# A mixer, cross-attention and feed-forward layer on one core: the last two quarters' output projection starts before the last mixer is done, and the feed-forward's token combinations are made later

## The chip, the cores and the metric

The kernel runs on one core of one Trainium2 chip. The metric is the time of one execution in device microseconds (us); lower is better. The core has a tensor engine (PE, with its weight loads shown as PEld), a vector engine (DVE), a scalar engine (ACT), GpSimd (POOL, nearly unused here) and SyncE (SP), whose queue issues all DMAs of this kernel. Each engine takes its own instructions in order and waits where one needs a result of another engine.

## What is computed

One layer of a decoder on 2048 tokens of 1024 channels, in float32. A mixer (a gated linear recurrence, "lru", beside a convolution module, "conf") feeds one output projection; then come cross-attention to 256 memory tokens and a gated feed-forward with a short convolution.

```
h = rms_norm(x, mix_norm_g);  z = h @ w_in
lru_x, lru_gate, conf_a, conf_b = split(z)                 # 512 channels each
y_lru = rg_lru(causal_dwconv(lru_x, 4 taps)) * gelu(lru_gate)
c = causal_dwconv(conf_a * sigmoid(conf_b), 31 taps)
c = silu(layer_norm(c))
x = x + concat([y_lru, c]) @ w_out
h = rms_norm(x, xa_norm_g);  m = rms_norm(mem, mem_norm_g)
x = x + softmax(h @ w_q @ k.T / 16) @ v @ w_o              # 4 heads, k and v from m @ w_kv
h = rms_norm(x, ffn_norm_g);  g, u = split(h @ w_up)       # 3072 channels each
x = x + (gelu(causal_dwconv(g, 3 taps)) * u) @ w_down
return rms_norm(x, final_norm_g)
```

## The kernel before

The tokens are cut into four quarters of 512 (q = 0 to 3; `TT` = 512, `NTB` = 4 blocks of 128 tokens). Every product is made of three matmuls on operands that are split into a high and a low part (names that end in h and l: `wh`, `wl`, `xh`, `xl`), each matmul 128x128 by 512 columns.

Per quarter there is a mixer (`mixer`, with `mix_norm`, `conf` and `lru`): normed tokens are turned by transposes against `ident`, multiplied by `W_in` (matmuls of `xh`, `xl` with `wh`, `wl`), and the gated product goes into `cb`, on which DVE runs 30 convolution steps (`conv<-cb`) for each of four channel blocks, 120 in all per quarter. The recurrence has its two gates (`gwa`, `gwx`), a scan, and its own convolution (`xc`). `normed` then does the layer norm over the 512 channels of `conv` (`conf_out`): a first sum (`sum<-sum,conv`) and a sum of squares (`sum<-sum,sq`), each followed on PE by one product with `ones`, a square root on ACT, and a `RECIPROCAL` of 512 columns on DVE.

Quarters 0 and 1 go through `attend` one by one: output projection (`yh`, `yl`), scores against the folded memory matrix (`xah`, `xal`), softmax (`prob`), and the second product (`pth`, `ptl`). Quarters 2 and 3 are done together by `attend_pair`, which makes each of its three products as a seven-step product of 2x2 blocks (`Folded.run`, after Strassen and Winograd; its seven steps are called products below). The rows of the blocks are the two quarters, the inner halves are lru and conf channels. The first two products (n = 0 and 1, operands A11 and A12) use quarter 2 alone; the third (n = 2, operand S2 = A21 + A22 - A11) is the first to use quarter 3. PE names their operands `hidh` and `hidl`. Sums of weight blocks for it are made on DVE by `Folds.prepare` (`wd<-wh,wl` and `t<-wd`), with `FOLD_PACE`.

The feed-forward's up product is of the same kind over token halves. For the first half of the tokens, `HalfX.kept` loads normed tokens (`xn`), makes four combinations of each of four channel blocks on DVE (16 instructions, `t<-xn` and `t<-xn,t`), and stores them.

What sets the order: each part is a generator that records operations and yields a pause, in units of PE work recorded so far; `drive` steps the first task in the list `TURNS` that is due. A planner (`Program.emit`) then gives every operation a due time, worked back from PE's recorded order, simulates the engines with a table of costs, and writes out a fixed order for each engine. So a pause (`MIX_WAIT`, `MIX_PACE`, `ATT_PACE`, `FOLD_PACE`, `T_PACE`, the numbers in `NORMED`) or a place in `TURNS` moves instructions on all engines at once. PE has eight banks (`ps`) to write to.

Of the kernel before, what the change touches and what calls it, by code (L numbers as in the profile page):

```python
# [23 lines left out]
NQ = S // TT  # L24
# [393 lines left out]
def hybrid_layer(  # L418
# [350 lines left out]
    def conf(X, C, pb, row, pace):  # L769
        for c in (0, 2):  # L770
            if pb is None:
                pb = yield from project(W_in, 3 * DL + c * P, X, pace)
            sg = []
            for j in range(2):
                t = tmp("sg")
                ACT(t[:], scaled("sg", pb[j], row)[:], AF.Sigmoid)
                sg.append(scaled("sg", t, row))
            pb = None
            yield 0
            pa = yield from project(W_in, 2 * DL + c * P, X, pace)  # L780
            cbs = []
            for j in range(2):
                cb = pr.new("D", (P, CK - 1 + TT), name="cb")
                V("tensor_copy", cb[:, : CK - 1], ctail[c + j][:])
                V("tensor_tensor", cb[:, CK - 1 :], pa[j][:], sg[j][:], op=ALU.mult)
                V("tensor_copy", ctail[c + j][:], cb[:, TT : TT + CK - 1])
                cbs.append(cb)
            for j in range(2):
                a, cb, w = tmp("conv"), cbs[j], vec["v512"][:, c + j, :]
                ACT(a[:], cb[:, 0:TT], AF.Identity, scale=w[:, I_CCW : I_CCW + 1], bias=w[:, I_CCB : I_CCB + 1])  # L790
                for t in range(1, CK):
                    V("scalar_tensor_tensor", a[:], cb[:, t : t + TT], w[:, I_CCW + t : I_CCW + t + 1], a[:], op0=ALU.mult, op1=ALU.add)
                C.append(a)
            yield 0
# [36 lines left out]
    def lru(q, X, L, row, pace):  # L831
        for c in (0, 2):
            pz = yield from project(W_in, c * P, X, pace)
            H = []
            for j in range(2):
                w = vec["v512"][:, c + j, :]
                zt = ztail[c + j]
                xc, z = tmp("xc"), scaled("z", pz[j], row)
                ACT(xc[:], z[:], AF.Identity, scale=w[:, I_LCW + 3 : I_LCW + 4], bias=w[:, I_LCB : I_LCB + 1])
                if row is None and q in Z_COPIED:  # L840
                    z = tmp("z")
                    ACT(z[:], pz[j][:], AF.Copy)
                for s in range(1, LK):
                    wt = w[:, I_LCW + 3 - s : I_LCW + 4 - s]
                    V("scalar_tensor_tensor", xc[:, s:], z[:, : TT - s], wt, xc[:, s:], op0=ALU.mult, op1=ALU.add)
                    V("scalar_tensor_tensor", xc[:, :s], zt[:, LK - 1 - s :], wt, xc[:, :s], op0=ALU.mult, op1=ALU.add)
                V("tensor_copy", zt[:], z[:, TT - LK + 1 :])
                H.append(xc)
            yield GATES
            for j in range(2):  # L850
                w = vec["v512"][:, c + j, :]
                xc = H[j]
                rt = []
                xh, xl = pair("x")
                split(xc[:], xh, xl)
                cs = slice((c + j) * P, (c + j + 1) * P)
                for (gh, gl), bi in zip(gates, (I_BA, I_BX)):
                    p = ps()
                    with together():
                        mm3(p[:], gh[:, cs], gl[:, cs], xh[:], xl[:], True, True)  # L860
                    t = tmp("gate")
                    ACT(t[:], p[:], AF.Sigmoid, bias=w[:, bi : bi + 1])
                    rt.append(t)
                r, i = rt
                V("tensor_tensor", i[:], i[:], xc[:], op=ALU.mult)
                a, m = xc, tmp("m")
                sp = nsp[:, c + j : c + j + 1]
                ACT(a[:], r[:], AF.Exp, scale=sp)
                ACT(r[:], r[:], AF.Tanh, scale=sp)
                ACT(m[:], a[:], AF.Square)  # L870

                V("scalar_tensor_tensor", m[:], m[:], 1.0, r[:], op0=ALU.add, op1=ALU.mult)
                ACT(m[:], m[:], AF.Sqrt, scale=-1.0)
                V("tensor_tensor", i[:], i[:], m[:], op=ALU.mult)
                V("tensor_tensor_scan", r[:], a[:], i[:], hlast[c + j][:], op0=ALU.mult, op1=ALU.add)
                V("tensor_copy", hlast[c + j][:], r[:, TT - 1 : TT])
                H[j] = r
            pg = yield from project(W_in, DL + c * P, X, pace)
            for j in range(2):
                ge = tmp("gelu")  # L880
                ACT(ge[:], scaled("gelu", pg[j], row)[:], AF.Gelu_apprx_tanh)
                V("tensor_tensor", ge[:], H[j][:], ge[:], op=ALU.mult)
                if q in FOLDED:
                    L.append(ge)
                    continue
                hi, lo = pair("y")
                split(ge[:], hi, lo)
                L.append((hi, lo))
            yield 0
# [156 lines left out]
    mixed = [None] * NQ  # L1046
    started = [Task(None) for _ in range(NQ)]
    attended = [Task(None) for _ in range(NQ)]
    turned_x = [Task(None) for _ in range(NQ)]
    x2_kept = Kept("x2", NQ * NTB * 2, F32)  # L1050
    xn_kept = Kept("xn", NQ * NK, F32)

# [12 lines left out]
    def mixer(q, after):  # L1065
        if after:
            yield after
            yield MIX_WAIT[q]
        if q == 0:
            X, pb, row = yield from first_tokens()  # L1070
        else:
            X, pb, row = (yield from mix_norm(q)), None, None
        C, L = [], []
        yield from conf(X, C, pb, row, MIX_PACE[q])
        yield from lru(q, X, L, row, MIX_PACE[q])
        del X, row
        mixed[q] = C, L

    def first_tokens():

# [182 lines left out]
    class HalfX:  # L1263
# [14 lines left out]
        def kept(self, ready, wait):  # L1278

            keys = ("T2", "T1", "T3", "T4")  # L1280
            k = Kept(f"tx{self.h}", 4 * KH, F32)
            yield ready
            for i in range(KH):
                b = {key: self.one(key, i) for key in ("B11", "B12", "B22")}
                t1 = combine("t", b["B12"][:], b["B11"][:], ALU.subtract)
                t2 = combine("t", b["B22"][:], t1[:], ALU.subtract)
                k.put(i, t2[:])
                k.put(KH + i, t1[:])
                yield wait
                t3 = combine("t", b["B22"][:], b["B12"][:], ALU.subtract)  # L1290
                t4 = combine("t", self.one("B21", i)[:], t2[:], ALU.subtract)
                k.put(2 * KH + i, t3[:])
                k.put(3 * KH + i, t4[:])
                del b, t1, t2, t3, t4
                yield wait
            for n, key in enumerate(keys):
                self.t[key] = lambda n=n: [k.get(n * KH + i) for i in range(KH)]
# [354 lines left out]
                yield from self.step(n, banks, start, into)  # L1652
                after(n)

    def attend_pair(ready):
        for t in ready:
            yield t
        q0 = FOLDED[0]
# [1 line left out]
        src = {}  # L1660
        x1_kept = Kept("x1", 4 * NTB, F32)

        def nothing(n):
            return ()

        def residual(load, store, st):
            acc = {}
# [34 lines left out]
        def operands(th):  # L1702
            Y, L = mixed[q0 + th]
            src[th, 0], src[th, 1] = L, Y

        operands(0)
        operands(1)
        st1 = [Stats(), Stats()]
        acc, add = residual(load_one, lambda th, tb, half, t: x1_kept.put((th * NTB + tb) * 2 + half, t[:]), st1)
        xsrc, posts = {}, [None, None]  # L1710
# [12 lines left out]
                posts[th] = spawn(normalise(acc, th, st1, PAIR_WAIT[0], take_xa(th)), me)  # L1723

        yield F_out.done
        yield from Folded(src, F_out, add).run(nothing, after1)
        del acc, add


# [128 lines left out]
        vec["v3072"] = columns([ffn_conv_w[0], ffn_conv_b], DFF, "v3072")  # L1858

    EARLY, VO_WAIT, V_LATE, Z_COPIED = 5, 2, 500, (0, 1)  # L1860
    MIX_WAIT, MIX_TURN, LN_SUM, LN_SQ, GATES = (1, 13, 0, 0), 6, 7, 1, 4
    MIX_PACE, ATT_PACE = (0, 4, 6, 4), ((0, 3, 0), (0, 0, 6), (7, 1, 1), (4, 0, 6))
    PAUSE = 2
    MEM_WAIT, VO_LATE, ATT_TURN, FFN_TURN, X_PACE, T_PACE = 0, 11, 1, (5, 0, 17, 5), 6, 2

    FOLDED = (2, 3)
    PAIR_WAIT, PAIR_TURN, FOLD_PACE = (1, 0, 9, 15), 5, (15, 6, 40)
    EARLY_AT = 4
    FOLD_AT = lambda: ([turned_x[0]], [mem_a, turned_x[1]], [mem_vo])
    F_out, F_a, F_vo = Folds(W_out, "t_out"), Folds(A_rows, "t_a"), Folds(VO_rows, "t_vo")  # L1870

    NORMED = [lambda: ([m[0]], 111), lambda: ([attended[0]], 33), lambda: ([m[2]], 2), lambda: ([m[3], n[2]], 0)]
    ATTEND = [lambda: [n[0]], lambda: [n[1]]]
    TURNS = lambda: [later, m[0], first_t, m[3], n[1], first, mem_a, fold, m[1], a[0], n[0], mem_vo, m[2], n[2], n[3], a[1], a[2], tail]
    X = [HalfX(h) for h in range(NH)]

    def first_x():
# [26 lines left out]
    m, n, a = mixers, normeds, attends  # L1904
# [3 lines left out]
        if q not in FOLDED:  # L1908
            a[q].gen = attend(q, ATTEND[q]())
    a[3] = a[2]  # L1910
    a[2].gen = attend_pair([n[2], n[3], attended[1]])
    fold = Task(fold_weights())
    later.gen, mem_a.gen, mem_vo.gen = setup_later(), memory_a(), memory_vo()
    first_t.gen, first.gen, tail.gen = X[0].kept(a[1], T_PACE), first_x(), feed_forward()
# [34 lines left out]
```

## Time and profile before

| | |
|---|---|
| median of 3 runs | 2457.88 us (2457.01 to 2458.15) |
| the profiled execution | 2455.91 us |
| its span, first to last instruction | 2454.1 us |
| mean granted PE clock | 0.996 |
| PE busy | 99% of the span, 11068 instructions |
| DVE busy | 80% |
| ACT busy | 51% |
| DMA | 566.78 MB, 231 GB/s in the mean |

The span holds, in order: the first three mixers with the memory products and the first quarter's attention (to about 650 us), the last mixer among the second quarter's second product (to about 823 us), the pair of quarters 2 and 3 (to about 1072 us), and the feed-forward. A busy PE is not PE at its peak, since its matmuls are pipelined; a place where it is held up shows in the view of waits, in the start times of the timeline, or as a stretch in which PE's count is low. Nearly all instructions are recorded through one helper, so the line is L394 everywhere, and the names of the tiles tell the place.

### The profile page before, as it was taken

How to read it: one execution, taken by the hardware profiler on the slowest of the kernel's cores; microseconds unless marked ns; L12 is line 12 of the kernel's file. 1: busy time of each engine (PE TensorE's matmuls, PEld its weight loads, DVE VectorE, ACT ScalarE, POOL GpSimd, SP SyncE). 2: the span in 40 equal slices, each digit the busy share in tenths (PEclk: the TensorE clock that was granted, in tenths of full speed). 3: DMA queues.
4: the chain of work that ended last, by engine and by line, in shares of the span. 5: the costliest groups of instructions: out<-in, count | busy, mean ns of one | idle time of the engine just before them, and what ended most of it. 6: DMA issues, size and time to landing. Idle time of an engine off the chain costs nothing. (4 is left out here: it accounts for less than half of the span.)

```text
span 2454.1 us, 33077 instructions
## 1 busy us (share of the span) xinstructions
PE 2422.9 (99%) x11068; PEld 2014.0 (82%) x11068; DVE 1974.7 (80%) x3297; ACT 1248.6 (51%) x2189; POOL 0.7 (0%) x6
## 2 busy tenths in 40 slices
PE   9999999999999799999999999999999999999998
PEld 8898888888787688888888888888888888888887
DVE  7999994399789978879888788987886675667656
ACT  6762665335925678685545445555454431225223
POOL 0000000000000000000000000000000000000000
PEclk9999999999999899999999999999999999999999
DMA  9688688786886965877554455444542487779775
GB/s 321 212 296 326 204 296 286 255 298 224 311 276 206 315 231 194 284 274 254 200 202 171 149 178 180 163 172 151 184 149 83 125 293 252 255 252 353 237 254 176
DMA packets 340416, 566.78 MB, mean 231 GB/s; under 512 B 32988, under 2 KB 110812, under 8 KB 340246
## 3 DMA queue, kind: packets, MB, share of 16 engines
q1 hardware_dynamic: 340246, 564.68, 67.4%
q8 instruction: 87, 1.43, 0.2%
q14 instruction: 83, 0.68, 0.1%
HBM read 403.07 MB, written 161.48 MB: 230 GB/s over the span
## 5 line engine op out<-in xcount | busy, mean ns | idle before, releaser
L394 PE MATMUL ps<-Xh,wh 128*128 128x512 f32 x1344 | 523.0, 389 | 0.0
L394 PE MATMUL ps<-Xl,wh 128*128 128x512 f32 x1344 | 522.9, 389 | 0.0
L394 PE MATMUL ps<-Xh,wl 128*128 128x512 f32 x1344 | 522.8, 389 | 0.0
L394 PE MATMUL ps<-wh,hidh 128*128 128x512 f32 x1008 | 394.2, 391 | 0.0
L394 PE MATMUL ps<-wl,hidh 128*128 128x512 f32 x1008 | 392.9, 390 | 0.0
L394 PE MATMUL ps<-wh,hidl 128*128 128x512 f32 x1008 | 392.8, 390 | 0.0
L394 DVE SCALAR_TENSOR_TENSOR conv<-cb,v,conv 128x512 f32<-128x512 f32 x480 | 339.5, 756 | 2.4 <-ACT conv L394 1.3
L394 PEld LDWEIGHTS ps<-Xh,wh 128*128 128x128 f32 x1344 | 252.3, 188 | 52.6 <-DVE up L394 0.2
L394 PEld LDWEIGHTS ps<-Xl,wh 128*128 128x128 f32 x1344 | 252.3, 188 | 52.5
L394 PEld LDWEIGHTS ps<-Xh,wl 128*128 128x128 f32 x1344 | 252.2, 188 | 52.3
L394 DVE TENSOR_TENSOR acc<-acc,ps 128x512 f32<-128x512 f32 x224 | 151.0, 687 | 152.3 <-PE ps L394 149.6
L394 PEld LDWEIGHTS ps<-wh,hidh 128*128 128x128 f32 x1008 | 189.7, 188 | 39.9 <-ACT gelu L394 0.5
L394 PEld LDWEIGHTS ps<-wl,hidh 128*128 128x128 f32 x1008 | 189.6, 188 | 39.7 <-issue 0.5
L394 PEld LDWEIGHTS ps<-wh,hidl 128*128 128x128 f32 x1008 | 189.6, 188 | 39.5
L394 PE MATMUL ps<-xh,wh 128*128 128x512 f32 x512 | 203.5, 397 | 0.0
L394 PE MATMUL ps<-xh,wl 128*128 128x512 f32 x512 | 199.5, 390 | 0.0
L394 PE MATMUL ps<-xl,wh 128*128 128x512 f32 x512 | 199.4, 389 | 0.0
L394 ACT ACTIVATE hidh<-s 128x512 fp32r<-128x512 f32 x144 | 87.8, 630 | 189.1 <-DVE s L394 134.3
L394 ACT ACTIVATE wh<-s 128x512 fp32r<-128x512 f32 x192 | 119.7, 628 | 107.7 <-DVE s L394 80.3
L394 ACT ACTIVATE wh<-raw 128x512 fp32r<-128x512 f32 x208 | 127.9, 627 | 74.1 <-PE ps L394 32.2
L394 DVE TENSOR_TENSOR wl<-raw,wh 128x512 fp32r<-128x512 f32 x208 | 141.8, 692 | 20.0 <-ACT wh L394 18.3
L394 ACT ACTIVATE u<-ps 128x512 f32<-128x512 f32 x144 | 85.9, 597 | 135.7 <-PE ps L394 133.7
(239 smaller groups left out, 3884.8 us busy)
## 6 DMA issues: line engine op xcount, KB each, us to landing
raw<-in_w_up_dram SPq DMA_DIRECT2D x96, 512.0 KB
wh<-w_down SPq DMA_DIRECT2D x164, 256.0 KB
wl<-w_down SPq DMA_DIRECT2D x164, 256.0 KB
wh<-w_in SPq DMA_DIRECT2D x96, 256.0 KB
wl<-w_in SPq DMA_DIRECT2D x96, 256.0 KB
hid<-cv SPq DMA_DIRECT2D x48, 512.0 KB
h<-hid SPq DMA_DIRECT2D x96, 256.0 KB
w_down<-wh SPq DMA_DIRECT2D x84, 256.0 KB
```

The lines of the kernel that those rows point to most:

```text
L394: getattr(e, name)(*[resolve(a) for a in args], **{k: resolve(a) for k, a in kw.items()})
```

## The change

`attend_pair` is released when quarter 2 is normed and quarter 1 attended; it waits for mixers 2 and 3 and for quarter 3's `normed` only before its third product (`more`, in `before1`). `HalfX.kept` of the first half waits in addition until the pair reaches its seventh product (`pair_begun`, set at `KEPT_AT` = 6). `mixer` publishes its lists C and L before they are filled, so that the parts are at hand as they are made. `convolved` is set but read nowhere. Beside these, the pauses and the list `TURNS` have new values: `m[3]` stands third in the list, `n[3]` and `n[2]` ahead of `fold`, `T_PACE` is 10 for 2, `FOLD_PACE` (7, 4, 33) for (15, 6, 40), and so on. The number of instructions is unchanged on PE, DVE and SP; on ACT 6 fewer table loads stand in the program (72 for 78).

```diff
@@ -1046,7 +1046,8 @@
     mixed = [None] * NQ
     started = [Task(None) for _ in range(NQ)]
     attended = [Task(None) for _ in range(NQ)]
-    turned_x = [Task(None) for _ in range(NQ)]
+    turned_x, convolved = ([Task(None) for _ in range(NQ)] for _ in range(2))
+    pair_begun = Task(None)
     x2_kept = Kept("x2", NQ * NTB * 2, F32)
     xn_kept = Kept("xn", NQ * NK, F32)
 
@@ -1070,11 +1071,10 @@
             X, pb, row = yield from first_tokens()
         else:
             X, pb, row = (yield from mix_norm(q)), None, None
-        C, L = [], []
+        C, L = mixed[q] = [], []
         yield from conf(X, C, pb, row, MIX_PACE[q])
+        convolved[q].done = True
         yield from lru(q, X, L, row, MIX_PACE[q])
-        del X, row
-        mixed[q] = C, L
 
     def first_tokens():
 
@@ -1280,6 +1280,8 @@
             keys = ("T2", "T1", "T3", "T4")
             k = Kept(f"tx{self.h}", 4 * KH, F32)
             yield ready
+            if not self.h:
+                yield pair_begun
             for i in range(KH):
                 b = {key: self.one(key, i) for key in ("B11", "B12", "B22")}
                 t1 = combine("t", b["B12"][:], b["B11"][:], ALU.subtract)
@@ -1652,7 +1654,7 @@
                 yield from self.step(n, banks, start, into)
                 after(n)
 
-    def attend_pair(ready):
+    def attend_pair(ready, more):
         for t in ready:
             yield t
         q0 = FOLDED[0]
@@ -1660,8 +1662,13 @@
         src = {}
         x1_kept = Kept("x1", 4 * NTB, F32)
 
-        def nothing(n):
-            return ()
+        def before1(n):
+            if n == 2:
+                for t in more:
+                    yield t
+                operands(1)
+            if n == KEPT_AT:
+                pair_begun.done = True
 
         def residual(load, store, st):
             acc = {}
@@ -1704,7 +1711,6 @@
             src[th, 0], src[th, 1] = L, Y
 
         operands(0)
-        operands(1)
         st1 = [Stats(), Stats()]
         acc, add = residual(load_one, lambda th, tb, half, t: x1_kept.put((th * NTB + tb) * 2 + half, t[:]), st1)
         xsrc, posts = {}, [None, None]
@@ -1723,7 +1729,7 @@
                 posts[th] = spawn(normalise(acc, th, st1, PAIR_WAIT[0], take_xa(th)), me)
 
         yield F_out.done
-        yield from Folded(src, F_out, add).run(nothing, after1)
+        yield from Folded(src, F_out, add).run(before1, after1)
         del acc, add
 
 
@@ -1858,20 +1864,20 @@
         vec["v3072"] = columns([ffn_conv_w[0], ffn_conv_b], DFF, "v3072")
 
     EARLY, VO_WAIT, V_LATE, Z_COPIED = 5, 2, 500, (0, 1)
-    MIX_WAIT, MIX_TURN, LN_SUM, LN_SQ, GATES = (1, 13, 0, 0), 6, 7, 1, 4
-    MIX_PACE, ATT_PACE = (0, 4, 6, 4), ((0, 3, 0), (0, 0, 6), (7, 1, 1), (4, 0, 6))
+    MIX_WAIT, MIX_TURN, LN_SUM, LN_SQ, GATES = (0, 9, 5, 0), 4, 5, 0, 5
+    MIX_PACE, ATT_PACE = (2, 4, 3, 4), ((1, 3, 0), (0, 0, 0), (10, 0, 4), (2, 4, 2))
     PAUSE = 2
-    MEM_WAIT, VO_LATE, ATT_TURN, FFN_TURN, X_PACE, T_PACE = 0, 11, 1, (5, 0, 17, 5), 6, 2
+    MEM_WAIT, VO_LATE, ATT_TURN, FFN_TURN, X_PACE, T_PACE = 18, 11, 1, (4, 6, 4, 11), 3, 10
 
     FOLDED = (2, 3)
-    PAIR_WAIT, PAIR_TURN, FOLD_PACE = (1, 0, 9, 15), 5, (15, 6, 40)
-    EARLY_AT = 4
+    PAIR_WAIT, PAIR_TURN, FOLD_PACE = (0, 0, 9, 15), 7, (7, 4, 33)
+    EARLY_AT, KEPT_AT = 6, 6
     FOLD_AT = lambda: ([turned_x[0]], [mem_a, turned_x[1]], [mem_vo])
     F_out, F_a, F_vo = Folds(W_out, "t_out"), Folds(A_rows, "t_a"), Folds(VO_rows, "t_vo")
 
-    NORMED = [lambda: ([m[0]], 111), lambda: ([attended[0]], 33), lambda: ([m[2]], 2), lambda: ([m[3], n[2]], 0)]
+    NORMED = [lambda: ([m[0]], 108), lambda: ([attended[0]], 30), lambda: ([m[2]], 19), lambda: ([m[3], n[2]], 4)]
     ATTEND = [lambda: [n[0]], lambda: [n[1]]]
-    TURNS = lambda: [later, m[0], first_t, m[3], n[1], first, mem_a, fold, m[1], a[0], n[0], mem_vo, m[2], n[2], n[3], a[1], a[2], tail]
+    TURNS = lambda: [later, m[0], m[3], first_t, mem_a, n[1], n[3], n[2], fold, m[1], a[0], n[0], mem_vo, first, m[2], a[1], a[2], tail]
     X = [HalfX(h) for h in range(NH)]
 
     def first_x():
@@ -1908,7 +1914,7 @@
         if q not in FOLDED:
             a[q].gen = attend(q, ATTEND[q]())
     a[3] = a[2]
-    a[2].gen = attend_pair([n[2], n[3], attended[1]])
+    a[2].gen = attend_pair([n[2], attended[1]], [m[2], m[3], n[3]])
     fold = Task(fold_weights())
     later.gen, mem_a.gen, mem_vo.gen = setup_later(), memory_a(), memory_vo()
     first_t.gen, first.gen, tail.gen = X[0].kept(a[1], T_PACE), first_x(), feed_forward()
```

The order of instructions moves throughout the first 1100 us. Three places follow.

PE, at the layer norm of quarter 3. Before, the two products with `ones` stood in a row behind the last input matmuls of mixer 3, and ahead of the pair's first product:

```order
L394 MATMUL ps<-xh,wl 128x512
L394 MATMUL ps<-sum,ones 128x512 x2
L394 MATMUL ps<-wh,hidh 128x512
L394 MATMUL ps<-wl,hidh 128x512
L394 MATMUL ps<-wh,hidl 128x512
```

In the change they stand apart, among the second quarter's second product. The first of them:

```order
L394 MATMUL ps<-wl,pth 128x512
L394 MATMUL ps<-wh,ptl 128x512
L394 MATMUL ps<-sum,ones 128x512
L394 MATMUL ps<-wh,pth 128x512
L394 MATMUL ps<-wl,pth 128x512
```

And the pair's first product, behind the last of that product's matmuls:

```order
L394 MATMUL ps<-wh,pth 128x512
L394 MATMUL ps<-wl,pth 128x512
L394 MATMUL ps<-wh,ptl 128x512
L394 MATMUL ps<-wh,hidh 128x512
L394 MATMUL ps<-wl,hidh 128x512
```

Between the first and the second product with `ones` stand 36 matmuls of `pth` and `ptl` now, and between the second and the pair's first product 54.

DVE, at the last sums of squares of quarter 3 (`sum<-sum,sq`). Before, the token combinations stood right behind them, and eight more of them ahead:

```order
L394 TENSOR_TENSOR sum<-sum,sq 128x512
L394 TENSOR_TENSOR hidl<-gelu,hidh 128x512
L394 TENSOR_TENSOR sum<-sum,sq 128x512
L394 TENSOR_TENSOR hidl<-gelu,hidh 128x512
L394 TENSOR_TENSOR sum<-sum,sq 128x512
L394 TENSOR_TENSOR t<-xn 128x512
L394 TENSOR_TENSOR t<-xn,t 128x512
L394 TENSOR_TENSOR t<-xn 128x512
L394 TENSOR_TENSOR t<-xn,t 128x512 x2
L394 TENSOR_TENSOR hidl<-conv,hidh 128x512 x4
L394 TENSOR_TENSOR t<-xn,t 128x512
L394 RECIPROCAL r<-r 128x512
```

In the change none stands there; the sum of a residual and the splits of gated products are between them, and the first token combination comes some 90 rows later:

```order
L394 TENSOR_TENSOR sum<-sum,sq 128x512
L394 TENSOR_TENSOR x_5015<-x_5015,ps 128x512
L394 TENSOR_TENSOR sum<-sum,sq 128x512
L394 COPY hlast<-gate 128x1
L394 TENSOR_TENSOR gelu<-gate,gelu 128x512
L394 TENSOR_TENSOR sum<-sum,sq 128x512
L394 TENSOR_TENSOR hidl<-gelu,hidh 128x512 x2
L394 COPY hlast<-gate 128x1
L394 TENSOR_TENSOR wd<-wh,wl 128x512
L394 COPY ctail<-cb 128x30
L394 TENSOR_TENSOR t<-wd,t 128x512
```

PE, at the end of the second quarter's score product. Before, the 32 transposes of mixer 3's tokens stood there:

```order
L394 MATMUL ps<-wh,xal 128x512
L394 MATMUL ps<-ident,x 128x128 x32
L394 MATMUL ps<-sum,ones 128x512
L394 MATMUL ps<-xh,wh 128x512
L394 MATMUL ps<-xl,wh 128x512
```

In the change those transposes stand among the second quarter's first output projection, and between the score product and the softmax's transposes stand 24 input matmuls of mixer 3, with 24 more behind:

```order
L394 MATMUL ps<-xl,wh 128x512
L394 MATMUL ps<-xh,wl 128x512
L394 MATMUL ps<-ident,prob 128x128 x16
L394 MATMUL ps<-xh,wh 128x512
L394 MATMUL ps<-xl,wh 128x512
```

## The prediction

> **What bounds the kernel now.** The page comes first: TensorE (PE) is shown busy for 99% of the span.
>
> ```profile
> span 2454.1 us, 33077 instructions
> PE 2422.9 (99%) x11068; PEld 2014.0 (82%) x11068; DVE 1974.7 (80%) x3297; ACT 1248.6 (51%) x2189; POOL 0.7 (0%) x6
> ```
>
> By this row at most 2454.1 - 2422.9 = 31.2 us could go, and the number of matmuls does not change. So the question is where PE is held up, and which of these places the new order touches. The view of stretches tells them apart; its columns are length, then busy time and count for PE, PEld, DVE, ACT and POOL, then PE's granted clock, DMA share and GB/s.
>
> ```profile
> 51.40:650.00 598.60, 597.22 (x2875) 501.34 (x2876) 509.64 (x892) 330.06 (x589) 0.00 (x0) 1.00 0.78 271
> 689.35:822.69 133.34, 118.09 (x530) 96.65 (x528) 132.27 (x222) 67.30 (x103) 0.00 (x0) 0.96 0.75 257
> 822.69:860.00 37.31, 37.17 (x150) 29.74 (x151) 37.31 (x60) 19.58 (x35) 0.00 (x0) 0.93 0.84 285
> 830.00:2440.00 1610.00, 1610.00 (x7202) 1335.86 (x7201) 1257.20 (x2035) 776.09 (x1350) 0.00 (x0) 1.00 0.62 209
> ```
>
> The first 650 us and everything from 830 us on are full. In 689 to 823 us the vector engine (DVE) is full instead (132.3 of 133.3 us) and PE is not. That is the last mixer's stretch. PE's waits there, and in the stretch of 640 to 660 us before it (last two rows), are these:
>
> ```profile
> PE ps L394 <- DVE sum L394: 11.6, 1, 11.6
> PE ps L394 <- ACT xn L394: 2.0, 4, 1.1
> PE ps L394 <- DVE xl L394: 1.3, 1, 1.3
> PE ps L394 <- DMA wh<-VO: 1.9, 1, 1.9
> PE ps L394 <- ACT prob L394: 1.8, 3, 0.9
> ```
>
> The Trainium skill ("Trainium Kernel Development and Optimization", Performance Expectations) holds that busy time of matmuls is a poor measure, because they are pipelined, and that weight-load busy time is a good one. Here weight loads fill 1335.86/1610 = 83% of the undisturbed stretch and 82% of the span; by that rule an estimate of the loss is 2454.1 - 2014.0/0.83 = 28 us, close to what is counted below.
>
> **Term 1, the last mixer's stretch.** PE's and DVE's groups in 689.3 to 822.7 us, and DVE's first and last instruction in it:
>
> ```profile
> L394 PE MATMUL ps<-xh,wh 128*128 128x512 f32 x100 | 39.4, 394 | 0.0
> L394 PE MATMUL ps<-wh,pth 128*128 128x512 f32 x52 | 20.3, 391 | 0.0
> L394 PE MATMUL ps<-ident,xn 128*128 128x128 f32 x32 | 6.0, 335 | 2.2 <-ACT xn L394 2.0 <-ACT gate L394 0.2
> L394 PE MATMUL ps<-xh,gwah 128*128 128x512 f32 x4 | 1.7, 417 | 0.2 <-ACT xh L394 0.2
> L394 DVE SCALAR_TENSOR_TENSOR conv<-cb,v,conv 128x512 f32<-128x512 f32 x120 | 82.6, 749 | 0.8 <-ACT conv L394 0.7
> ...
> 689.35 0.69 DVE L394 TENSOR_TENSOR cb<-ps,sg 128x512 f32<-128x512 f32 x1 [7.50 <-PE ps L394]
> 821.99 0.70 DVE L394 TENSOR_TENSOR sum<-sum,sq 128x512 f32<-128x512 f32 x1
> ```
>
> DVE waits 7.50 us for the first gated product of the last mixer, then works without a break for 133.3 us until the last sum of squares, for which PE is waiting. PE's own work in that time is smaller. Matmuls of 512 columns start 0.23 us apart, transposes some 0.11 us (16 in 1.91 us, the last one's end included), a DVE tensor-tensor step takes 0.60 us, a convolution step up to 0.69 (82.6/120 above), a row maximum 0.69:
>
> ```profile
> 774.57 0.39 PE L394 MATMUL ps<-xh,wh 128*128 128x512 f32 x1
> 774.80 0.39 PE L394 MATMUL ps<-xl,wh 128*128 128x512 f32 x1
> 775.26 1.91 PE L394 MATMUL ps<-ident,xn 128*128 128x128 f32 x16
> 810.16 1.02 PE L394 MATMUL ps<-sum,ones 128*128 128x512 f32 x2
> 646.77 0.69 DVE L394 TENSOR_REDUCE smalls<-ps 128x2 f32<-128x512 f32 x1
> 823.79 0.70 DVE L394 TENSOR_TENSOR t<-xn 128x512 f32<-128x512 f32 x1
> 824.39 1.30 DVE L394 TENSOR_TENSOR t<-xn,t 128x512 f32<-128x512 f32 x2
> ```
>
> In the old order there stand 300 input-projection matmuls, 156 of the second quarter's last product (pth, ptl) and 24 of the gates: 480 x 0.227 = 109.0 us. With 48 transposes (5.3) and one sum (0.9) it is 115.2 us. PE loses 133.3 - 115.2 = 18.1 us.
>
> In the new order mixer 3 starts earlier, so the same stretch, from its first gated product to the second sum, holds 300 + 180 (score product, xa) + 138 (pth, ptl) + 24 = 642 matmuls, 145.7 us; with 32 transposes (3.5) and a sum (0.9) 150.1 us. DVE's share grows too, from 221 instructions to 262. Out go 8 token combinations (t<-xn), 4 residual sums, 2 splits; in come 13 more weight sums (wd), 12 more differences of these, 4 more splits, 2 more gate products: 17 x 0.60 = 10.2 us; 8 row maxima add 5.4 and 16 small ones some 1.6. So DVE needs 133.3 + 17.2 = 150.5 us against PE's 150.1: the debt of 18.1 us falls to 0.4. But the balance is even, so each wait of DVE in this stretch now comes through to PE. Lower bound 0, where DVE's surplus is hidden by small waits of PE elsewhere. Upper bound from the softmax, whose instructions now stand inside the stretch and waited like this before it:
>
> ```profile
> 642.57 0.17 DVE L394 TENSOR_TENSOR smalls<-smalls 128x4 f32<-128x4 f32 x1 [3.96 <-ACT junk L394]
> 652.99 0.17 DVE L394 RECIPROCAL smalls<-smalls 128x2 f32<-128x2 f32 x1 [1.15 <-ACT prob L394]
> 654.66 0.75 DVE L394 SCALAR_TENSOR_TENSOR xl<-ps,v,xh 128x512 fp32r<-128x512 f32 x1 [0.92 <-ACT xh L394]
> ```
>
> With the smaller ones between them this is about 8 us. I take 3.0 us, nearer the low end, since the new order puts convolution steps between the softmax's steps, which the old one had not there. Term 1: -18.1 + 3.0 = -15.1.
>
> **Term 2, the slow restart.** After the wait of 11.65 us the matmuls come at half pace:
>
> ```profile
> 822.83 2.04 PE L394 MATMUL ps<-sum,ones 128*128 128x512 f32 x2 [11.65 <-DVE sum L394]
> 823.89 1.41 PE L394 MATMUL ps<-wh,hidh 128*128 128x512 f32 x1
> ...
> 828.39 0.40 PE L394 MATMUL ps<-wh,hidh 128*128 128x512 f32 x1
> ```
>
> Ten matmuls, nine steps in 4.50 us where 2.04 would do: 2.5 us lost, the clock of 0.93 in the third stretch. No wait of 1 to 2 us shows this. With term 1's wait it goes: -2.5. The Trainium skill ("TensorE: Matmul & The Clock Gate", Part 1) has an idle window of some 3.4 us halve the clock and about as much busy time restore it; that would price the restart at 3.4 x 0.5 = 1.7 us, an estimate that would put the result 0.8 us higher. The trace agrees in kind, with 2.5 us; by that rule, too, a remaining wait of 3 us in one piece costs no restart.
>
> **Term 3, the transposes at 650 us.** They wait three times for softmax results, then for weights:
>
> ```profile
> 650.21 1.91 PE L394 MATMUL ps<-ident,x 128*128 128x128 f32 x16
> 658.26 1.13 PE L394 MATMUL ps<-sum,ones 128*128 128x512 f32 x2 [1.94 <-DMA wh<-VO]
> 658.82 0.79 PE L394 MATMUL ps<-xh,wh 128*128 128x512 f32 x1
> 659.45 0.40 PE L394 MATMUL ps<-xl,wh 128*128 128x512 f32 x1
> ```
>
> 32 transposes need 3.5 of the 8.05 us between the first two rows: 4.5 lost, and 0.4 more at the step of 0.63. In the new order mixer 3's transposes are done long before, among the first output projection. Behind the score product stand 24 input matmuls (5.4 us) before the softmax's transposes, and 24 more behind those. So -4.9, and 0.5 back for the new place (0 to 4.9).
>
> **Parts that I cost at nothing.** The pair's first two products no longer wait for mixer 3, but product 3, which does, stands behind 54 + 96 matmuls and 32 transposes, 37.6 us after the second sum (old: 96 matmuls, 21.8). DVE's way from the last sum of squares to the fourth split of the S2 operands ends here:
>
> ```profile
> 845.41 1.90 DVE L394 TENSOR_TENSOR hidl<-s,hidh 128x512 fp32r<-128x512 f32 x3
> ```
>
> From 822.7 to 847.3 that was about 25 us; it has two instructions more now, 1.2 us: some 11 us of cover. If that cover went, the excess would come as a wait before product 3. The 16 token combinations move behind, into the pair's later products: 9.6 us of DVE, where DVE is full until 860 us but has an eighth to a quarter of its time free after:
>
> ```profile
> 850.00:900.00 50.00, 50.00 (x238) 41.83 (x237) 44.18 (x77) 34.60 (x72) 0.00 (x0) 1.00 0.86 291
> 900.00:950.00 50.00, 50.00 (x238) 41.93 (x237) 37.32 (x67) 40.02 (x83) 0.00 (x0) 1.00 0.49 158
> ```
>
> Without cover they cost up to 9.6 us. Their loads and stores on SP's queue number as before. The other moves (memory products and W_out among the second mixer, to 640 us) stay in a stretch that loses little either way: +0.5, within -3 to +4.
>
> **Sum.** 2454.1 - 15.1 - 2.5 - 4.9 + 0.5 + 0.5 = 2432.6 us of span. The median of the runs lies 3.8 us over the span: 2436.4, and I say 2436.5.
>
> **Rivals.** (a) The debt moves rather than goes: DVE's waits in the softmax come through whole, 8 us in place of 3, and in a piece long enough for a slow restart (2.5): 2436.5 + 5 + 2.5 = 2444. For it speaks the even balance of 150.5 against 150.1; against it that convolution steps are at hand to fill. (b) Everything small goes as well: no wait in the stretch, and 3 us of those in the first 640: 2436.5 - 6 = 2430.5. (c) The change does not do what it says: the sum is still late by as much, since some chain that ACT or DMA sets, not DVE's work, ended that wait. Then 2457. Against it: DVE has 132.27 busy of 133.34 us. (d) Slower: DVE takes its instructions in order, and 15 weight sums that need fresh loads now stand among the convolutions; each blocks them if its load is late. Waits for such loads are these, the first over the whole span, the second in 560 to 900 us:
>
> ```profile
> DVE t L394 <- DMA wd<-in_w_out_dram: 14.8, 3, 7.3
> DVE wd L394 <- DMA wl<-A: 0.3, 1, 0.3
> ```
>
> At 7.3 us each, four make 29 us on top of the even balance in place of 3, and with the restart kept (2.5) the run takes 2436.5 + 26 + 2.5 = 2465. It decides from about 22 us of such waits on; the second row, the same kind of sum in the same phase, speaks against it.
>
> **Chances.** Forecast 0.70, (a) 0.14, (b) 0.07, (c) 0.03, (d) 0.06. The range reaches from (b) past (a), 2430 to 2448; the ends of the unknown costs, 3 us down and 8 up, lie inside. A change of 0.2% (5 us) is about what this measurement can tell: faster 0.91, the same 0.03, slower 0.06.
>
> **What would show it.** Right: no PE wait over 3 us behind the sums of mixer 3, no matmuls at 0.43 us behind them, the granted clock at 1.00 there, DVE full through this stretch, and fewer transposes that wait for prob. The weakest step is the 3.0 us: a longer wait at mixer 3's sums or at the transposes of the second quarter's probabilities means (a). A wait at product 3, for s or hid, would show that the later coverage is wrong. DVE waits for DMA before wd mean (d). A gain under 15 us would say that the stretch was not bound by DVE's amount of work.

## The result, and the profile after

| | before | after |
|---|---|---|
| median of 4 runs each | 2457.45 us (2455.34 to 2458.15) | 2430.69 us (2430.26 to 2433.14) |
| the profiled execution | 2455.91 us | 2431.12 us |
| its span | 2454.1 us | 2429.3 us |
| mean granted PE clock | 0.996 | 0.999 |

The changed kernel is faster: ratio 0.9895, 95% interval 0.9877 to 0.9912, 26.8 us between the medians. The page's head shows the same work in a shorter span (PE still busy for 99%):

```profile
span 2429.3 us, 33082 instructions
PE 2415.3 (99%) x11068; PEld 2010.7 (83%) x11068; DVE 1970.7 (81%) x3297; ACT 1241.7 (51%) x2183; POOL 0.7 (0%) x6
```

Stretches of the changed kernel (columns as in the prediction). The first runs from the last mixer's first gated product to the second sum, the second is what follows that sum:

```profile
635.88:785.01 149.13, 146.99 (x660) 120.80 (x659) 148.78 (x265) 69.43 (x127) 0.00 (x0) 1.00 0.77 263
785.01:822.00 36.99, 36.99 (x179) 30.84 (x178) 31.74 (x54) 29.34 (x54) 0.00 (x0) 1.00 0.88 293
```

The last mixer's stretch is 149.13 us long, DVE is still full in it (148.78), and now PE is nearly full too (146.99; before 118.09 of 133.34). Behind the sum the granted clock is 1.00 where it was 0.93. What is left of PE's waits, in the whole execution (two more are of 0.5 us and less):

```profile
PE ps L394 <- DMA raw<-in_ffn_norm_g_dram: 3.3, 1, 3.3
PE ps L394 <- DVE ptl L394: 1.9, 1, 1.9
PE ps L394 <- ACT mem L394: 1.3, 1, 1.3
```

The row `DVE sum` of 11.6 us is gone, and so are the rows for `xn` and `prob`. PE's timeline at the two sums of the last layer norm has no idle time before either:

```profile
775.83 1.12 PE L394 MATMUL ps<-sum,ones 128*128 128x512 f32 x2
...
785.01 1.02 PE L394 MATMUL ps<-sum,ones 128*128 128x512 f32 x2
```

They stand 9.2 us apart, and 36 matmuls fill that time (8.2 us at 0.227, and 0.9 for the sum). Before they stood at 810.16 and 822.83 us, 12.7 apart, with nothing between them. This distance turned out to be the largest single part of the matter.

### The profile page after: what moved, and what is told of

It reads as the page before. It is cut to its first block, busy times and chain, and to the rows that moved or that the text cites. A ratio compares the mean times of both kernels' runs of the same rounds, so it can differ in the third digit from the quotient of the medians.

```text
span 2429.3 us, 33082 instructions
## 1 busy us (share of the span) xinstructions
PE 2415.3 (99%) x11068; PEld 2010.7 (83%) x11068; DVE 1970.7 (81%) x3297; ACT 1241.7 (51%) x2183; POOL 0.7 (0%) x6
## 5 line engine op out<-in xcount | busy, mean ns | idle before, releaser
L394 DVE TENSOR_TENSOR wl<-s,wh 128x512 fp32r<-128x512 f32 x192 | 131.7, 690 | 30.2 <-ACT wh L394 21.4
```

The source lines that it names most:

```text
L394: getattr(e, name)(*[resolve(a) for a in args], **{k: resolve(a) for k, a in kw.items()})
```

## The experiments

The names: `old_...` is the kernel before with an edit, `new_...` the changed kernel with one. In all of them the kernel before ran beside; its medians were 2456.4 to 2457.4 us.

**1. Is the old order bound by DVE's amount of work?** `old_less_conv` skips 27 of the last mixer's 120 convolution steps as the program is written out, and leaves the order as it is (these values are then missing from the output).

```diff
+                if o.mark and o.mark * 9 % 40 < 9:
+                    continue
```

> The old order with 27 of the last mixer's 120 convolution steps left out (that part of the result is then not computed); every other instruction and the order of all engines as before. Theory (amount of DVE work between the last mixer's first gated product and its last sum of squares sets PE's wait): DVE's 133.3 us shrink by 27 x 0.66 = 17.9 us to PE's own 115.2, the slow restart (2.5 us) goes too, and 3 to 6 us come back before the pair's third product: 2442 us, 2437 to 2447. Rival (that wait is ended by a chain over ACT or a transfer, DVE only looks full): within 3 us of the old kernel's 2457.

Measured: 2457.46 us (2453.96 to 2462.41), ratio 1.0000 (0.9991 to 1.0010). The rival's number. 27 x 0.69 = 18.6 us of DVE work are gone, and PE waits as long for the sum. Its view of waits:

```profile
PE ps L397 <- DVE sum L397: 11.1, 1, 11.1
```

And a stretch of the mixer in which DVE was busy for 20.00 of 20 us before:

```profile
720.00:740.00 20.00, 20.00 (x90) 16.57 (x89) 16.57 (x27) 1.63 (x2) 0.00 (x0) 1.00 0.56 196
```

So the theory of the prediction fell for the old order: DVE's full 133 us were real, but they were not what kept PE waiting.

**2. Does DVE's amount bind in the new order?** `new_dose12` and `new_dose40` put 12 and 40 clears of a spare tile behind every tenth and every third convolution step of the last mixer; `new_less_conv` leaves out the same 27 steps as above.

```diff
+                if o.mark and o.mark * 1 % 10 < 1:
+                    self.nc.vector.memset(self.extra_tile[:], 0.0)
```

> The changed kernel with 12 clears of an unused tile of 128x512 (0.40 us each, 4.8 us in all) spread over the last mixer's convolution steps on DVE; nothing else moves. In the changed kernel's trace DVE is full from 635.9 to 784.1 us and PE takes the second product with ones 0.9 us after the last sum of squares. Theory (even balance): all but 0.9 us comes through, 3.5 to 5 us slower, 2434 to 2436. Rival (DVE has room there): under 1.5 us.

> As the dose of 12, with 40 clears, 16.1 us of DVE work. Theory: 15 us come through, and a wait that long in one piece brings the slow restart (2.5 us) again if it is not cut up into short waits: 2445 to 2449. Rival: under 5 us, since the planner left slack between the sums and the third product.

> The changed kernel with 27 of the last mixer's 120 convolution steps left out (that part of the result is then not computed). Theory: only the wait for ptl (1.9 us) and a gate wait of 0.2 still hang on DVE there: 1.5 to 3 us faster, 2428 to 2429. Rival (the stretch still holds a debt that is spread in small waits): 8 us or more faster.

Measured: 2436.48 (2436.02 to 2437.74), 2448.32 (2448.17 to 2451.36) and 2429.36 us (2429.04 to 2429.63): +5.8, +17.6 and -1.3 against the change's 2430.69. The first and the last lie just outside what was expected. On DVE the stretch from the first gated product to the last sum of squares takes 148.4 us in the change, and 153.3 and 165.6 with the clears, so the doses are 4.9 and 17.3 us: added work comes through about one to one, removed work gives little. PE does not lose this time at the sums (`new_dose12` has no wait there) but in waits spread over the stretch and in slow matmuls behind them. The new order stands close to the balance of the two engines that the prediction worked out.

**3. What ends the wait in the old order?** Between the first sum and the second stands a chain: the mean is taken off four blocks (`conv<-conv,ps`), ACT squares them, DVE adds the squares. DVE's timeline of the kernel before in that time:

```profile
811.83 0.68 DVE L394 TENSOR_TENSOR conv<-conv,ps 128x512 f32<-128x512 f32 x1
812.43 1.29 DVE L394 SCALAR_TENSOR_TENSOR m<-m,gate 128x512 f32<-128x512 f32 x2
813.63 1.88 DVE L394 TENSOR_TENSOR conv<-conv,ps 128x512 f32<-128x512 f32 x3
815.42 0.69 DVE L394 TENSOR_TENSOR hidl<-gelu,hidh 128x512 fp32r<-128x512 f32 x1
816.03 1.30 DVE L394 TENSOR_TENSOR gate<-gate,m 128x512 f32<-128x512 f32 x2
817.23 2.46 DVE L394 TENSOR_TENSOR_SCAN gate<-xc,hlast,gate 128x512 f32<-128x512 f32 x2
819.60 0.68 DVE L394 TENSOR_TENSOR sum<-sum,sq 128x512 f32<-128x512 f32 x1
```

From 811.83 to the last sum's end at 822.69 it is 10.9 us, all of it full on DVE: 7 steps of the chain itself (7 x 0.60 = 4.2), and 6.7 of the recurrence and of splits that stand among them in DVE's order. PE has nothing in its order for that time. The new theory: **PE waits because its two sums stand next to each other, as long as this chain takes**; what DVE did earlier counts only where it makes the first sum late. Three runs tried it, all without the 27 steps, so that DVE's amount ahead of the first sum is out of the way (values are missing from the output).

`old_less_tail` also skips the 8 token combinations that stand between the last x product and the second sum; GpSimd clears their tiles, so the output lacks them too:

```diff
+                if o.mark == -1:
+                    token += 1
+                    if token <= 8:
+                        self.nc.gpsimd.memset(...)
+                        continue
```

> The old order, without 27 conv steps (as in old_less_conv), and without the 8 token combinations (8 x 0.60 = 4.8 us of DVE) that stand between the last x product and the second sum of the last mixer; GpSimd clears their tiles instead. Theory A (the amount of DVE's work behind the last x product sets the sum): 4.8 us less than old_less_conv, 2452.5 (2451 to 2454). Theory B (the sums of squares stand on DVE behind the last gates' products and scans, and these come at the end of a chain over PE, ACT and DVE from the x product, which has only about 0.4 us of slack): 0.6 to 1.5 us less, 2456 (2455 to 2457.5).

Measured: 2456.67 us (2454.93 to 2457.91), ratio 0.9995 (0.9986 to 1.0004), where theory B put it. PE's timeline, then DVE's:

```profile
809.87 1.02 PE L404 MATMUL ps<-sum,ones 128*128 128x512 f32 x2
821.93 2.04 PE L404 MATMUL ps<-sum,ones 128*128 128x512 f32 x2 [11.04 <-DVE sum L404]
```

```profile
810.93 0.69 DVE L404 TENSOR_TENSOR conv<-conv,ps 128x512 f32<-128x512 f32 x1 [3.92 <-PE ps L404]
```

DVE is now early and idles 3.92 us for PE's first sum, and PE still waits 11.04 for the second. An engine that idles right ahead of the wait is not late by its amount of work.

`old_less_tail_moved` has in addition the last gates' 2 products and 2 scans (3.6 us) behind the three sums of squares instead of ahead of them:

```diff
+            if o.mark == -3:
+                held.append(o)
+                continue
+            yield o
+            if squares == 3:
+                yield from held
+                held = []
+                squares = 9
```

> As old_less_tail, and the last two gates' products and scans (4 DVE instructions, 3.6 us) are moved from ahead of the last mixer's three sums of squares to behind them. Theory B (chain of the gates, with the sums of squares behind it in DVE's order): the sums come free of the chain, 5 to 6 us less than old_less_conv, 2452 (2450 to 2453.5), so this move gains about 4 where the 8 combinations alone gain about 1. Theory A (amount alone): both gain, 4.8 and 3.6, 2449 (2447.5 to 2450.5).

Measured: 2458.77 us (2455.23 to 2460.03), ratio 1.0001 (0.9992 to 1.0011): a miss for both. The wait did what the chain says; the time did not follow. PE's timeline:

```profile
814.35 1.02 PE L417 MATMUL ps<-sum,ones 128*128 128x512 f32 x2
823.05 2.04 PE L417 MATMUL ps<-sum,ones 128*128 128x512 f32 x2 [7.67 <-DVE sum L417]
...
849.34 0.50 PE L417 MATMUL ps<-wl,hidh 128*128 128x512 f32 x1 [0.65 <-DVE wl L417]
851.75 0.79 PE L417 MATMUL ps<-wl,hidh 128*128 128x512 f32 x1 [1.44 <-DVE wl L417]
```

The wait is 3.4 us shorter (11.04 to 7.67) for 3.6 us of steps moved out of the chain. But PE waits 2.1 us for weight splits at the third product, behind the moved steps, and in the profiled execution it came 4.5 us later to the first sum (814.35 against 809.87), in a part where the two programs are alike. So the wait speaks for the chain. The time decides nothing: the two medians differ by 2.1 us, with the ranges of the runs overlapping.

`old_tail_dose` puts 12 clears on DVE into the first sum itself (without the 27 steps, but with the token combinations):

```diff
+                if o.mark == 120:
+                    for _ in range(12):
+                        self.nc.vector.memset(self.extra_tile[:], 0.0)
```

> The old order, without 27 of the last mixer's 120 conv steps (as in old_less_conv), and with 12 clears of a 128x512 tile (about 0.40 us each, 4.8 us) put on DVE behind the first sum of the last mixer, that is behind its last x product. Theory (the wait is set by what stands on DVE behind the last x product, and no longer by the amount before it): 4.8 us longer than old_less_conv, 2462 (2460.5 to 2463.5). Rival (a chain over ACT or a transfer ends the wait, with DVE at its side): the clears are hidden, 2457 to 2459.

Measured: 2465.28 us (2463.02 to 2468.39), ratio 1.0032 (1.0021 to 1.0043), 7.8 more than `old_less_conv`. The direction is the theory's, and the size was wrong because the dose was: in a row the clears come 0.66 us apart (DVE's timeline, the first two and the step behind the last), 7.6 us in all and not 4.8.

```profile
807.58 0.48 DVE L397 MEMSET extra<- 128x512 f32 x1
808.24 0.48 DVE L397 MEMSET extra<- 128x512 f32 x1 [0.17 <-DVE extra L397]
...
815.22 0.63 DVE L401 TENSOR_TENSOR sum<-sum,conv 128x512 f32<-128x512 f32 x1
```

PE's timeline shows a wait for the first sum that was not there, and the wait for the second a little longer than the 11.10 of `old_less_conv`:

```profile
817.80 2.04 PE L401 MATMUL ps<-sum,ones 128*128 128x512 f32 x2 [5.06 <-DVE sum L401]
832.31 2.04 PE L401 MATMUL ps<-sum,ones 128*128 128x512 f32 x2 [12.47 <-DVE sum L401]
```

The two make up 6.4 of the 7.8 us; where the rest goes is not shown. DVE work at the first sum costs about its full time, and nothing is won by taking work away earlier in the mixer.

**4. Which part of the change does it?** Two answers need no run. With the new numbers, `attend_pair` put back to waiting for all of mixers 2 and 3 at its start gives the same instructions in the same order on every engine as the change; so does the old list `TURNS`. The edit that the change is named for moves nothing here: in both orders the pair's first product stands behind the second sum of quarter 3 (in the change it starts at 798.15 us, the sum at 785.01). The others:

`old_numbers_new_code`: all of the code, with the old numbers. `old_mixpace_new`: the old code, with only `MIX_PACE` new. `new_old_pace`: the change, with the line of `MIX_PACE` and `ATT_PACE` old. `new_early_tokens`: the change, without the wait for `pair_begun`. `old_late_tokens`: the old kernel, with that wait alone.

```diff
-    MIX_PACE, ATT_PACE = (2, 4, 3, 4), ((1, 3, 0), (0, 0, 0), (10, 0, 4), (2, 4, 2))
+    MIX_PACE, ATT_PACE = (0, 4, 6, 4), ((0, 3, 0), (0, 0, 6), (7, 1, 1), (4, 0, 6))
```

(That is `new_old_pace`; the two with tokens take out, or put in, the lines `if not self.h: yield pair_begun`.)

> The change's code (the pair begins before quarter 3 is done, token combinations wait for the pair) with all pauses at the old values. By the order 96 matmuls of the pair's first two products then stand inside the last mixer, but the third product stands right behind the second sum. Theory: DVE's work up to the third product's operands is 153.5 us by instruction lengths (154.3 before), PE's 137, so the wait moves from the sum to the third product and stays: 2456 us, 2451 to 2460. Rival (starting the pair early is what fills the wait): 2434 to 2440.

> The old code with one pause changed: the mixers' pace from (0, 4, 6, 4) to (2, 4, 3, 4). By the order the last mixer's stretch then holds 141 us of PE work against 142.7 us of DVE work by instruction lengths (147 us by the old trace's ratio), and 50 us of PE work lie between the second sum and the third product. Theory (the last mixer starts earlier and is spread over more PE work): most of the gain, 2440 us, 2433 to 2447. Rival (the two edits of the code carry the gain): 2452 to 2458.

> The changed kernel without the wait of the token combinations for the pair. PE's order is the same; DVE's combinations still stand behind the last mixer's sums, earlier among the pair's products. Theory: they meet spare time of DVE: within 2 us of the changed kernel, 2429 to 2433. Rival (making them later is a part of the gain): 5 to 10 us slower, 2436 to 2441.

> The old code and pauses, with the token combinations held back until the pair's seventh product, the one part of the change alone. By the order DVE's work up to the third product's operands falls from 154.3 to 148.0 us by instruction lengths, PE's stays at 137. Theory: 6.5 us faster, 2451, 2447 to 2454. Rival (this part alone removes the sum's wait): 2440 or less.

> The changed kernel with the one line of the mixers' and attentions' paces (MIX_PACE, ATT_PACE) put back to the old numbers. Theory (the new pauses work as a set: they set how much PE work lies behind the last x product and behind the second sum): the third product comes directly behind the second sum again, and most of the gain is gone, 2450 (2444 to 2458). Rival (the later token combinations and the other numbers carry the gain): 2431 to 2437.

The table gives the time, the matmuls (M) and transposes (T) that PE's order has between the two sums and from the second sum to the third product, and PE's wait at each of the two ends in the trace:

| | us | between the sums | wait | to the third product | wait |
|---|---|---|---|---|---|
| before | 2457.5 | 0 | 11.65 | 96 M | none |
| after | 2430.7 | 36 M | none | 150 M, 32 T | none |
| `new_early_tokens` | 2433.0 | 36 M | none | 150 M, 32 T | none |
| `old_late_tokens` | 2448.9 | 60 M | none | 48 M | 4.45 |
| `old_numbers_new_code` | 2461.7 | 24 M | none | 0 | 11.40 |
| `new_old_pace` | 2472.8 | 36 M | none | 0 | 14.21 |
| `old_mixpace_new` | 2468.0 | 36 M, 8 T | none | 204 M, 32 T | none |

Wherever PE has 24 matmuls or more between the sums, it does not wait for the second one. In `old_numbers_new_code`, where 24 are enough, the sums come 6.6 us apart:

```profile
830.34 1.02 PE L394 MATMUL ps<-sum,ones 128*128 128x512 f32 x2
836.94 1.12 PE L394 MATMUL ps<-sum,ones 128*128 128x512 f32 x2
...
849.47 0.79 PE L394 MATMUL ps<-wh,hidh 128*128 128x512 f32 x1 [11.40 <-ACT hidh L394]
```

But then the same wait stands one step on: the pair's first two products were used up ahead of the sums, and nothing is left to cover the way from the second sum to the third product (a square root, a reciprocal, the norm and the splits), which takes 12.5 us here. That is why the code alone gives nothing (ratio 1.0017, 1.0007 to 1.0026; 2461.70 us, 1.7 over the end of the range expected, with the wait where the theory had it), and why the pauses of the mixers decide: `new_old_pace` has the cover between the sums and none behind them, and is slower than the kernel before (1.0059, 1.0044 to 1.0074). It was expected at 2444 to 2458 with the third product's wait, and missed that: the wait came (14.21), and 9.8 us of others behind 640 us, for `x`, `xt` and `xh` (4.5, 3.0, 2.3), beside it. `old_late_tokens` fits its expectation (2448.94, ratio 0.9968, 0.9958 to 0.9978); but its one line moves PE's order as well, so this run alone does not tell the DVE time of the combinations from the 60 matmuls that now stand between the sums. `old_less_tail` helps: it takes eight of the combinations off DVE, leaves PE's order, and is only 0.8 us faster than `old_less_conv`, within the noise; that speaks for PE's order as what brought most of the gain here.

`old_mixpace_new` was a miss (2467.95, ratio 1.0044, 1.0030 to 1.0058; expected 2440). Both ends of the norm are covered there, and PE loses elsewhere:

```profile
PE ps L394 <- DVE wl L394: 5.3, 3, 2.0
PE ps L394 <- ACT xh L394: 5.0, 1, 5.0
PE ps L394 <- ACT xn L394: 4.2, 1, 4.2
PE ps L394 <- ACT wh L394: 3.4, 1, 3.4
```

So `MIX_PACE` alone does not carry the gain, and with the mixers' and attentions' paces put back it is lost. The other numbers were not tried one by one. `new_early_tokens` (2432.96, 2432.32 to 2433.38, ratio 0.9902, 0.9887 to 0.9916) is some 2 us slower than the change, with overlapping intervals: the later token combinations, the second half of the change's name, are worth about 2 us, if anything.

Not tried: the old order with nothing but its second sum moved 36 matmuls back. It is the cleanest test of the chain, and the runs above only surround it.

## Why the prediction was right, and where it was not

Faster was predicted, 2436.5 us in a range of 2430 to 2448; 2430.7 was measured, inside and near the low end.

**Term 1** (-18.1 + 3.0 = -15.1). The number held, its reason only in part. PE's lag behind its own work (the start of each matmul in the trace, less the sum of the paces ahead of it; the pace of a kind is the median step from its start to the next, 0.227 us for 512 columns, 0.109 for a transpose) grows in the changed stretch by 3.0 us, as taken, 2.2 of it in one wait for `ptl` at 763.69 us. In the old stretch it grew by 18.6. Only 11.8 of these belong to the wait for the sum; 2.1 were lost at the gates (800 to 802 us), and 4.8 at the transposes of `xn`, partly in waits and partly in slow steps (12 of them take 2.82 us here, where 16 took 1.91 in the prediction's rows):

```profile
778.30 0.33 PE L394 MATMUL ps<-ident,xn 128*128 128x128 f32 x1 [1.14 <-ACT xn L394]
...
780.72 2.82 PE L394 MATMUL ps<-ident,xn 128*128 128x128 f32 x12 [0.25 <-ACT gate L394]
```

The granted clock is 0.61 in 780 to 782 us and 0.53 in 782 to 784. In `old_less_conv`, with 27 of DVE's steps taken out, the three losses are 11.3, 2.0 and 4.7, so hardly any of them hung on the amount of DVE's work. The step that failed is "DVE's amount of work" as what ended the wait. Two bounds met in the old order within a microsecond: DVE's 133 us of work, and PE's way to the first sum plus the chain. The second alone was enough, as experiment 1 showed. That is close to rival (c) in its cause, though most of the chain is DVE's own steps behind the first sum and not ACT or a transfer, and it is not (c) in its time: the prediction let (c) mean that nothing changes, when the same new order also puts 36 matmuls into the gap. It did not count this cover; that the wait went all the same is luck. Had the order left the sums together, the forecast would by this account have missed a wait of some 11 us, with no row of its sum to show it. What the new order did about the other 6.9 us (gates and transposes) no run takes apart.

**The test that the prediction named** for this ("a gain under 15 us would say that the stretch was not bound by DVE's amount of work") was one-sided: a gain of 26.8 did not show the opposite.

**The balance of the new order**, 150.5 us of DVE against 150.1 of PE, was right for DVE: the stretch took 149.1, and the doses of experiment 2 came through whole. PE's share was counted too high: the trace has 624 matmuls in the stretch and not 642, so that PE's own work is 146.1 us, and the lag of 3.0 is the difference to 149.1. The prediction took its 3.0 for waits of the softmax, so that the two agree is luck in part. Rival (a), waits that come through and a slow restart, needed only some 5 us more on DVE: `new_dose12` has both.

**Term 2** (-2.5): the lag grew by 2.7 behind the old wait, and in the change by nothing behind the second sum. Right; but its remark that no wait of 1 to 2 us shows the slow pace overlooked the transposes of `xn` above, in its own trace. **Term 3** (-4.9, +0.5): the old lag grew by 4.7 at the transposes and the sum behind them (650 to 660 us), and the transposes' new place costs nothing. Right.

**Costed at nothing**: no wait at the third product, no load that blocks DVE beyond 0.4 us, so rival (d) is out. Correctly priced, but the pair's early start was not even made by its own edit.

**The sum.** The span fell by 24.8 instead of 21.5 us. By PE's lag, 15.6 come from term 1, 2.7 and 4.7 from the others, and 1.7 from the first 640 us. The prediction then put the median 3.9 us over the span, as it lay before; it lies 1.4 over it now. These 2.5 us and the 3.3 of span are the whole difference of 5.8. In a single execution the time lies 1.8 us over the span, before and after; the 3.8 before came from a profiled execution that was 2 us faster than the median, and to carry it over was a mistake.

## What to carry to other kernels

A full engine beside a waiting one may be a coincidence: skip some of its steps in the unchanged order, which costs one run, before its total goes into a sum. Where two reductions of a normalisation sit next to each other on an engine, count what stands between them on that engine and what the chain between them takes on the others, and do the same from the last one to the first consumer; cover given to one gap is easily taken from the other. And compare the orders before crediting an edit: here the edit in the title moved nothing once the pauses had been set.

## What was not expected of the hardware

How long PE waited does not tell whether its matmuls come slowly afterwards. PE's timeline in `new_dose12`, behind a wait of 2.74 us:

```profile
768.89 0.52 PE L395 MATMUL ps<-wh,ptl 128*128 128x512 f32 x1 [2.74 <-DMA wl<-VO]
769.23 0.61 PE L395 MATMUL ps<-wh,pth 128*128 128x512 f32 x1
...
772.62 0.41 PE L395 MATMUL ps<-wh,ptl 128*128 128x512 f32 x1
772.87 0.40 PE L395 MATMUL ps<-wh,pth 128*128 128x512 f32 x1
```

Eight matmuls start 0.42 us apart, 3.4 us in all, of which 8 x (0.42 - 0.227) = 1.6 are lost. The change's own wait of 1.85 us:

```profile
763.69 0.50 PE L394 MATMUL ps<-wh,ptl 128*128 128x512 f32 x1 [1.85 <-DVE ptl L394]
764.02 0.40 PE L394 MATMUL ps<-wh,pth 128*128 128x512 f32 x1
764.26 0.39 PE L394 MATMUL ps<-wl,pth 128*128 128x512 f32 x1
```

Here the steps are 0.33 and 0.24. But the length alone does not decide. Before, full pace follows the wait of 1.94 us at 658.26 us (the rows are in the prediction's term 3; the granted clock is 1.00). In `old_less_tail_moved` the same wait at the same place, again behind three short waits for `prob`, is followed by slow matmuls and a granted clock of 0.54 (660 to 662 us):

```profile
660.35 2.08 PE L417 MATMUL ps<-sum,ones 128*128 128x512 f32 x2 [1.94 <-DMA wh<-VO]
...
662.65 0.63 PE L417 MATMUL ps<-xl,wh 128*128 128x512 f32 x1
663.08 0.63 PE L417 MATMUL ps<-xh,wl 128*128 128x512 f32 x1
```

In `old_tail_dose` 1.52 us there were enough, and in `new_old_pace` 2.06 us at 799.65 us were not. What decides stays open. The Trainium skill ("TensorE: Matmul & The Clock Gate", Part 1) has an idle window of some 3.4 us bring the slow clock and about as much busy time end it. The second half agrees with the 3.4 us in `new_dose12`, while before the slow stretch lasted 5.6 us (822.83 to 828.39); the first does not agree with the 2.74 us there, and the prediction's remark that a wait of 3 us in one piece would cost no restart falls with it.

In the first row of `new_dose12` the wait is put down to a DMA, and a late DVE may stand behind it. DVE's weight sum `t` holds up its store on SP's queue, and loads of the second product's weights stand behind that store. SP's queue in the change:

```profile
740.23 0.42 SPq L394 DMA_DIRECT2D wl<-w_in  x1
744.57 0.32 SPq L394 DMA_DIRECT2D t_vo<-t  x1
746.54 0.32 SPq L394 DMA_DIRECT2D wh<-VO  x1
```

Its waits around that store, in the change (736 to 747 us) and in `new_dose12` (738 to 752 us):

```profile
SPq L394 <- DVE t L394: 3.8, 1, 3.8
```

```profile
SPq L395 <- DVE t L395: 5.7, 1, 5.7
```

In `new_dose12` the last load ahead of the store is issued 3.0 us later than in the change (743.19 us), the store and the first load behind it 4.8 us later (749.35 and 751.32). So here a vector engine that is late delays the transfers behind its store. That PE's 2.74 us come from this one store is argued from the order of the queue, not shown by a run.
